# Modulation work taken off GpSimd, and PSUM tiles of two banks, in a two-layer hybrid decoder trunk

## Chip, cores, metric

The kernel runs on one core of a Trainium2 chip. The metric is the device time in microseconds (us) of one execution, from inputs in device memory to the output written there. Lower is better. TensorE, VectorE, ScalarE, GpSimd and SyncE are the engines; in rows they are PE (PEld for its weight loads), DVE, ACT, POOL and SP.

## What is computed

Two layers over one sequence of 256 tokens with 1024 channels, in float32. Each layer has six modulation vectors of 1024 numbers, made from the condition vector `c`; then a mixer (a state space model, differential attention and block attention side by side), and an MLP with a hidden width of 4096:

```python
mod = silu_c @ w_ada[l] + b_ada[l]
sh1, sc1, g1, sh2, sc2, g2 = jnp.split(mod[:, None, :], 6, axis=-1)
h = rmsnorm(x, norm1_g[l]) * (1.0 + sc1) + sh1
proj = h @ w_in[l]
u, dq, dk, dv, mq, mk, mv = jnp.split(proj, splits, axis=-1)
...                                     # y_ssm, y_diff, y_moba
x = x + g1 * (jnp.concatenate([y_ssm, y_diff, y_moba], axis=-1) @ w_out[l])
h = rmsnorm(x, norm2_g[l]) * (1.0 + sc2) + sh2
x = x + g2 * (jnp.square(jax.nn.relu(h @ mlp_w1[l])) @ mlp_w2[l])
```

After the two layers `x` is normalized once more and multiplied by `final_g`.

## The kernel before

**Layout.** `x` stands transposed in SBUF as eight tiles `xT[k]` of 128 channels by 256 tokens. All large weights, 184 units of 128x1024 numbers (512 KB), are read once each, in the order of their use, on SyncE's DMA queue. `unit` (L112) brings one into the ring `raw` (three buffers), ScalarE copies its high part, rounded to the matmul's input format, into `whl` (L118; four buffers), and VectorE writes the rest, raw minus high, beside it (L119). `mm3` (L124, its matmul is L127) multiplies in three terms: high x high, high x low, low x high. So each unit costs a DMA, a ScalarE pass, a VectorE pass and TensorE's work.

**Modulation.** A vector is a sum over eight 128x1024 tiles of `w_ada`, each weighted by eight columns of `cs` (silu of `c`). The tiles come through the ring `ada` (four buffers), also on SyncE's queue (L255), between the raw units. The first two vectors of layer 0 are made at the start; ten come later, each by one of three ways. On TensorE, `ada_two` multiplies two tiles in a step (L250); `ada_finish` transposes the row into a column (L229). On VectorE, `ada_one` does one `scalar_tensor_tensor` per tile (L281; `adaacc` is the accumulator). With `gp`, ScalarE scales the tile (L275) and GpSimd adds it (L277). In the last two ways eight small matmuls sum the accumulator over the partitions (L286). Two vectors go over TensorE, five over VectorE (four from `ada_todo_dve`, one from `ada_todo_last`) and three over GpSimd.

**PSUM.** It has eight banks of 128x512 numbers: four tiles `acc` and four tiles `wk`, one bank each. Projections and the mixer's output accumulate in `acc`; transpositions, sums and other short things use `wk`.

**MLP.** It runs in two halves of 2048 hidden channels. In a half, eight calls of `mlp1_mm` produce a pair of hidden tiles each (two units, 48 matmuls, two `wk` tiles). `p_norm` multiplies each of the two by the row of token norms `rb` on VectorE (L465, 128x258: the last two columns carry the shift); `mlp1_act` does relu, square, the high copies (ScalarE) and the low subtractions (VectorE, L1018) into tiles of other names that are free then (`HID`: `mx`, `at_e`, `uT`, `g2`, `at_on`, `vv`). Then eight calls of `mlp2` each use two units and all 16 hidden tiles (L1035, L1041), in one `acc` tile, and add into `xT[f]` (L1044). In the second half `square_in` sums squares for the next norm on GpSimd (L1058, L1060), and in layer 0 `p_tile` (L450) prepares the next mixer's input; its two 128x2 columns are GpSimd's (L454, L455), its low part is VectorE's (L458).

**Order.** The program is written in the order of two strings `MIXER`, one for each layer's mixer: each word is a piece (P a modulation step on TensorE, D two on VectorE, G on GpSimd, S, Y, O the state space model, C, R, E, V, W, F the attentions, K the output projection). A scheduler then places instructions on their engines by priority; `:n` and `LATE` shift the priority of a piece or of modulation steps. Each engine, and SyncE's queue, runs its instructions in that order.

Of the kernel before, what the change touches and what calls it, by code (L numbers as in the profile page):

```python
# [56 lines left out]
def hybrid_trunk(ctx, tc, xT_d, pos_d, par_d, sb_d, sbt_d, scw_d, glu_d, wm_d, wa_d, out_d):  # L57
# [267 lines left out]

    ada_todo = [(l, i, k) for l, i in ADA_PE for k in range(0, 8, 2)]
    ada_todo_dve = [(l, i, k, 0) for l, i in ((0, 2), (1, 0), (1, 1), (1, 2)) for k in range(8)]
    ada_todo_gp = [(l, i, k, 1) for l, i in ((0, 5), (1, 3), (1, 4)) for k in range(8)]
    ada_todo_last = [(1, 5, k, 0) for k in range(8)]
# [53 lines left out]
    def x_ssq():  # L383

        qs = []
        for i in range(0, KT, 4):
# [996 lines left out]
```

## Time and profile before

| | |
|---|---|
| median of three runs | 711.23 us (710.13 to 718.77) |
| the profiled execution | 710.69 us, of which the span of the trace is 709.0 |
| TensorE busy | 668.0 us, 94% |
| VectorE busy | 565.3 us, 80% |
| ScalarE busy | 423.5 us, 60% |
| GpSimd busy | 96.4 us, 14% |

The span falls into five stages: the start (0 to 56 us: first modulation and first projections), the mixer of layer 0 (56 to 173), its MLP (173 to 393), the mixer of layer 1 (393 to 516) and its MLP (516 to 709). Times in the rows further down count from the start of the span. An engine's busy share is an average over stages with different limits, so rows by stage and the waits of the engine that is busiest are read beside it. "A <- B: total, times, longest" is the time in which A stood idle until B's instruction ended.

### The profile page before, as it was taken

What the parts mean: (1) busy time and instruction counts of PE and PEld (TensorE: products, weight loads), DVE (VectorE), ACT (ScalarE), POOL (GpSimd) and SP (SyncE); (2) the same over time, 40 slices, a digit from 0 to 9 for tenths busy, and PEclk for the clock granted to TensorE, in tenths of its full rate; (3) what the DMA queues carried; (4) which work ended last, traced back from release to release, by engine and by line L of the source; (5) the groups of instructions that cost most, each with busy time, mean ns of one, the idle gap of its engine ahead of it and who ended that gap; (6) DMA issues with size and microseconds to landing.
All of it is one profiled execution on the core that took longest, in us unless ns stands there. A gap on an engine that the chain in (4) does not pass through costs nothing.

```text
span 709.0 us, 13373 instructions
## 1 busy us (share of the span) xinstructions
PE 668.0 (94%) x5046; PEld 593.2 (84%) x5046; DVE 565.3 (80%) x1202; ACT 423.5 (60%) x789; POOL 96.4 (14%) x93
## 2 busy tenths in 40 slices
PE   8999999599999899979699999999999999999994
PEld 6686777588999789979599977788999988999884
DVE  6789989979999897889699888897786566666653
ACT  4568465556777853778544546556577733577540
POOL 0000000911132130134511000001000000000221
PEclk9899999989999999999899999999999999999998
DMA  9986867667787588877686352323455555555531
GB/s 327 395 293 239 307 226 282 242 198 255 241 298 242 184 297 284 315 258 260 252 277 218 122 179 91 124 91 114 149 167 188 178 176 184 183 183 190 188 119 61
DMA packets 42977, 151.98 MB, mean 214 GB/s; under 512 B 4896, under 2 KB 5024, under 8 KB 42912
## 3 DMA queue, kind: packets, MB, share of 16 engines
q1 hardware_dynamic: 42480, 150.60, 61.9%
q8 instruction: 40, 0.66, 0.4%
q10 hardware_dynamic: 432, 0.53, 0.2%
q14 instruction: 25, 0.20, 0.1%
HBM read 150.06 MB, written 1.05 MB: 213 GB/s over the span
## 4 chain that ended last, share of the span: by engine, by line
PE 53%; DVE 21%; DMA 12%; ACT 7%; issue 6%; POOL 1%; SPq 0%; DVEq 0%; ACTq 0%; POOLq 0%
PE wk L127 13%; PE acc L1041 12%; PE acc L127 8%; PE acc L1035 7%; DMA ada<-in_wa_dram 6%; DVE whl L119 6%; DMA raw<-in_wm_dram 4%; DVE adaacc L281 2%; ACT whl L118 2%; PE wk L886 1%; PE wk L286 1%; PE acc L1038 1%; DMA xall<-in_xT_dram 1%; PE acc L812 1%; PE acc L813 1%
## 5 line engine op out<-in xcount | busy, mean ns | idle before, releaser
L118 ACT ACTIVATE whl<-raw 128x1024 fp32r<-128x1024 f32 x184 | 193.8, 1056 | 161.3 <-PE acc L1035 62.9
L119 DVE TENSOR_TENSOR whl<-raw,whl 128x1024 fp32r<-128x1024 f32 x184 | 233.9, 1277 | 64.3 <-ACT whl L118 62.3
L127 PE MATMUL wk<-hx,whl 128*128 128x258 f32 x1536 | 189.9, 285 | 4.9 <-DVE whl L119 4.9
L127 PEld LDWEIGHTS wk<-hx,whl 128*128 128x128 f32 x1536 | 187.4, 191 | 7.2 <-DVE whl L119 5.3
L277 POOL TENSOR_TENSOR qT<-qT,ada 128x1024 f32<-128x1024 f32 x21 | 59.4, 2831 | 150.8 <-ACT ada L275 136.7
L1041 PE MATMUL acc<-mx,whl 128*128 128x512 f32 x240 | 63.6, 409 | 0.0
L281 DVE SCALAR_TENSOR_TENSOR adaacc<-ada,cs,adaacc 128x1024 f32<-128x1024 f32 x35 | 55.1, 1575 | 5.1 <-DMA ada<-in_wa_dram 5.1
L1041 PEld LDWEIGHTS acc<-mx,whl 128*128 128x128 f32 x240 | 45.0, 197 | 8.5
L127 PE MATMUL acc<-mx,whl 128*128 128x256 f32 x384 | 50.5, 289 | 0.0
L127 PEld LDWEIGHTS acc<-mx,whl 128*128 128x128 f32 x384 | 47.8, 194 | 1.6 <-issue 1.4
L1044 DVE SCALAR_TENSOR_TENSOR xall<-acc,mod,xall 128x256 f32<-128x256 f32 x62 | 29.8, 481 | 19.0 <-PE acc L1035 18.2
L127 PE MATMUL acc<-whl,hx 128*128 128x256 f32 x288 | 39.9, 286 | 0.0
L1011 ACT ACTIVATE sp_pa<-sp_pa 128x256 f32<-128x256 f32 x64 | 31.4, 498 | 14.0 <-DVE sp_pa L465 13.8
L812 PE MATMUL acc<-whl,hx 128*128 128x512 f32 x96 | 39.1, 407 | 0.3 <-DVE whl L119 0.3
L127 PEld LDWEIGHTS acc<-whl,hx 128*128 128x128 f32 x288 | 36.4, 189 | 2.8 <-issue 1.6
L813 PE MATMUL acc<-whl,hx 128*128 128x512 f32 x96 | 38.6, 402 | 0.0
L454 POOL CAST hx<-mod 128x2 fp32r<-128x2 f32 x24 | 10.3, 427 | 208.1 <-DVE at_ra L907 120.7
L811 PE MATMUL acc<-whl,hx 128*128 128x512 f32 x96 | 38.5, 406 | 0.0
L1035 PEld LDWEIGHTS acc<-mx,whl 128*128 128x128 f32 x256 | 34.8, 189 | 2.6
L1035 PE MATMUL acc<-mx,whl 128*128 128x256 f32 x256 | 35.6, 281 | 0.0
L465 DVE TENSOR_TENSOR sp_pa<-wk,rb 128x258 f32<-128x258 f32 x64 | 26.5, 419 | 9.2 <-PE wk L127 9.2
L1041 PE MATMUL acc<-at_e,whl 128*128 128x512 f32 x120 | 32.6, 393 | 0.0
(378 smaller groups left out, 1100.3 us busy)
## 6 DMA issues: line engine op xcount, KB each, us to landing
raw<-in_wm_dram SPq DMA_DIRECT2D x184, 512.0 KB, 4.1
ada<-in_wa_dram SPq DMA_DIRECT2D x90, 512.0 KB, 5.9
qT<-in_wa_dram SPq DMA_DIRECT2D x4, 512.0 KB, 8.2
xall<-in_xT_dram SPq DMA_DIRECT2D x4, 256.0 KB, 6.5
adaacc<-in_wa_dram SPq DMA_DIRECT2D x2, 512.0 KB, 9.3
sp_gc<-in_sbt_dram SPq DMA_DIRECT2D x2, 256.0 KB, 4.8
sp_gc<-in_scw_dram SPq DMA_DIRECT2D x2, 256.0 KB, 5.7
sb<-in_sb_dram SPq DMA_DIRECT2D x2, 256.0 KB, 5.1
```

Source lines behind the costliest of these rows:

```text
L118: A.activation(hi, w, AF.Copy)
L119: (eng or V).tensor_tensor(lo, w, hi.bitcast(F32), op=OP.subtract)
L127: last_mm[0] = T.matmul(out, a[:, p, :], b[:, q, :], start=start and i == 0, stop=stop and i == 2, skip_group_check=True)
L277: GP.tensor_tensor(acc, acc, w, op=OP.add)
L281: V.scalar_tensor_tensor(acc, w, c, acc, op0=OP.mult, op1=OP.add)
L811: T.matmul(o, h[:, 0, sl], w[:, 0, :], start=(k == 0), stop=False, skip_group_check=True)
L812: T.matmul(o, h[:, 0, sl], w[:, 1, :], start=False, stop=False, skip_group_check=True)
L813: last_mm[0] = T.matmul(o, h[:, 1, sl], w[:, 0, :], start=False, stop=last, skip_group_check=True)
L1011: A.activation(r[:, i, :S], r[:, i, :S], AF.Relu, bias=r[:, i, S:S + 1])
L1035: last_mm[0] = T.matmul(acc[:, :S], w[:, 1, sl], a[:, 0, :], start=False, stop=last, skip_group_check=True)
L1041: T.matmul(acc, w[:, 0, sl], a.rearrange("p c t -> p (c t)"), start=first, stop=False, skip_group_check=True)
L1044: V.scalar_tensor_tensor(xT[f], acc[:, c * S:(c + 1) * S], mvec(l, 5, f), xT[f], op0=OP.mult, op1=OP.add)
```

## The change

1. `ada_one` has no GpSimd way any more. Vectors (0,3), (0,4) and (1,4) go over TensorE, by steps of four tiles (`ada_four`); (0,2), (0,5), (1,0), (1,1), (1,2), (1,3) and (1,5) over VectorE. VectorE does 8 of its 56 steps in the first mixer, 32 in the MLP of layer 0 (24 before), 8 in the second mixer (none before) and 8 in the MLP of layer 1 (as before). Vector (1,4) on TensorE falls into the second mixer. `LATE` is 60 instead of 100.
2. `p_tile`'s two columns and `square_in`'s sums are VectorE's.
3. `acc` is two tiles of two banks. `mlp1_mm` accumulates a pair in one such tile, `mlp2` in a `wk` tile. `p_norm` is one instruction of 128x516 for a pair, and for 14 of 16 hidden tiles of a half the high copy and the low subtraction are one instruction for a pair, into tiles of double size.
4. The squares for the MLP's norm come first, their sums after the first row of `mlp1_mm`'s matmuls, the norm after the third.
5. The two `MIXER` strings are written in another order, with priorities.

```diff
     def acc_tile():
-        return psum.tile([128, 512], F32, name="acc")
+        return psum.tile([128, 2, 512], F32, name="acc", bufs=2)
...
-    ADA_PE = ((0, 3), (0, 4))
+    ADA_PE = ((0, 3), (0, 4), (1, 4))
...
-    def ada_two(l, i, k):
+    def ada_four(l, i, k):
...
         row = ada_st[l, i]
-        for j in range(2):
-            ada_mm(row, k + j, [ada_tile(l, i, k + j)])
-        if k == 6:
+        ws = [ada_tile(l, i, k + j) for j in range(4)]
+        for j in range(4):
+            ada_mm(row, k + j, ws[j:j + 1])
+        if k == 4:
             ada_fin.append(lambda: ada_finish(l, i, row))
...
-        if gp:
-            A.activation(w if k else acc, w, AF.Copy, scale=c)
-            if k:
-                GP.tensor_tensor(acc, acc, w, op=OP.add)
-        elif k == 0:
+        if k == 0:
             V.tensor_scalar(acc, w, c, None, op0=OP.mult)
         else:
             V.scalar_tensor_tensor(acc, w, c, acc, op0=OP.mult, op1=OP.add)
...
-        GP.tensor_copy(h[:, 0, S:], sh)
-        GP.tensor_tensor(h[:, 1, S:], sh, h[:, 0, S:].bitcast(F32), op=OP.subtract)
+        V.tensor_copy(h[:, 0, S:], sh)
+        V.tensor_tensor(h[:, 1, S:], sh, h[:, 0, S:].bitcast(F32), op=OP.subtract)
...
         t = work.tile([128, 2, SX], F32, name="sp_pa", bufs=2)
-        for i in range(2):
-            V.tensor_tensor(t[:, i], ps[i][:, :SX], rb, op=OP.mult)
+        V.tensor_tensor(t, ps[:, :, :SX], rb[:, None, :].to_broadcast([128, 2, SX]), op=OP.mult)
...
     def mlp1_mm(h, then=None):
-        ps = [wk_tile(), wk_tile()]
+        ps = acc_tile()
...
-            if then and (m, k) == (1, 2):
+            if then and m and k in then:
                 with tc.issue_after(last_mm[0].ins):
-                    then()
+                    then[k]()
...
+        if m < 14:
+            pool, n, bufs = HID[m // 2]
+            a = pool.tile([128, 2, 2, S], F32R, name=n, bufs=bufs)
+            last_act[0] = A.activation(a[:, :, 0, :], r, AF.Copy)
+            last_dve[0] = V.tensor_tensor(a[:, :, 1, :], r, a[:, :, 0, :].bitcast(F32), op=OP.subtract)
+            return [a[:, 0], a[:, 1]]
...
-        acc = acc_tile()
+        acc = wk_tile()
...
-            GP.tensor_scalar(sqsum[0], q, EPS * D / 128, None, op0=OP.add)
+            V.tensor_scalar(sqsum[0], q, EPS * D / 128, None, op0=OP.add)
         else:
-            GP.tensor_tensor(sqsum[0], sqsum[0], q, op=OP.add)
+            V.tensor_tensor(sqsum[0], sqsum[0], q, op=OP.add)
...
-    LATE = 100
+    LATE = 60
...
-    GP_STEPS = (1, 1, 1, 1, 2, 2, 2, 2, 1, 1, 1, 1, 2, 2, 0, 0)
-    V_STEPS = (1, 2, 2, 2, 2, 2, 2, 2, 2, 2, 2, 2, 1, 0, 0, 0)
+    V_STEPS = ((2, 2, 2, 2, 3, 3, 3, 3, 1, 1, 1, 1, 3, 3, 2, 0), (2, 2, 2, 2) + (0,) * 12)
```

The second word string begins, before and now, with "Rm S0 S1 C0 Y0 R0 E01" and "Rm:80 S0:-50 S1:10 C0 P1 Y0 R0 D1 Em0".

What moves on the engines is seen at two places. First, VectorE at the first pairs of the MLP of layer 0. Its rows before, from the end of the norm (L405 to L407 write `rb`) to the first hidden tiles (`mx`):

```order
L281 SCALAR_TENSOR_TENSOR adaacc<-ada,cs,adaacc 128x1024
L406 TENSOR_TENSOR so_y<-so_y,sq 128x256
L119 TENSOR_TENSOR whl<-raw,whl 128x1024
L407 SCALAR_TENSOR_TENSOR rb<-so_y,sq 128x256
L119 TENSOR_TENSOR whl<-raw,whl 128x1024
L465 TENSOR_TENSOR sp_pa<-wk,rb 128x258 x3
L119 TENSOR_TENSOR whl<-raw,whl 128x1024
L281 SCALAR_TENSOR_TENSOR adaacc<-ada,cs,adaacc 128x1024
L465 TENSOR_TENSOR sp_pa<-wk,rb 128x258
L1018 TENSOR_TENSOR mx_2333<-sp_pa,mx_2333 128x256
L1018 TENSOR_TENSOR mx_2336<-sp_pa,mx_2336 128x256
L281 SCALAR_TENSOR_TENSOR adaacc<-ada,cs,adaacc 128x1024
L465 TENSOR_TENSOR sp_pa<-wk,rb 128x258
```


and now (L278 is the modulation step, L409 to L411 the end of the norm, L468 `p_norm`, L1017 the subtraction):

```order
L409 SCALAR_TENSOR_TENSOR so_y<-wk,sq 128x256
L278 SCALAR_TENSOR_TENSOR adaacc<-ada,cs,adaacc 128x1024
L410 TENSOR_TENSOR so_y<-so_y,sq 128x256
L278 SCALAR_TENSOR_TENSOR adaacc<-ada,cs,adaacc 128x1024
L411 SCALAR_TENSOR_TENSOR rb<-so_y,sq 128x256
L119 TENSOR_TENSOR whl<-raw,whl 128x1024
L468 TENSOR_TENSOR sp_pa<-acc,rb 128x516
L119 TENSOR_TENSOR whl<-raw,whl 128x1024 x2
L1017 TENSOR_TENSOR mx_2305<-sp_pa,mx_2305 128x2x256
L468 TENSOR_TENSOR sp_pa<-acc,rb 128x516
L278 SCALAR_TENSOR_TENSOR adaacc<-ada,cs,adaacc 128x1024
L119 TENSOR_TENSOR whl<-raw,whl 128x1024
```


The pair's four VectorE instructions (two L465, two L1018) have become two of double size, in `acc` instead of `wk`, and between two norms there stand two steps and two weight subtractions.

Second, SyncE's queue from the end of the MLP of layer 0 into the second mixer. Its rows before, where L255 brings a modulation tile and L110 a unit of the large weights:

```order
L255 DMA ada<-in_wa_dram 128x1024 x2
L110 DMA raw<-in_wm_dram 128x1024
L255 DMA ada<-in_wa_dram 128x1024 x2
L110 DMA raw<-in_wm_dram 128x1024 x3
L255 DMA ada<-in_wa_dram 128x1024
L110 DMA raw<-in_wm_dram 128x1024 x93
```


and now, where the row of 18 units runs from the last three of the MLP of layer 0 to the fifteenth of the second mixer's 28:

```order
L255 DMA ada<-in_wa_dram 128x1024
L110 DMA raw<-in_wm_dram 128x1024 x18
L255 DMA ada<-in_wa_dram 128x1024 x6
L110 DMA raw<-in_wm_dram 128x1024 x3
L255 DMA ada<-in_wa_dram 128x1024 x4
L110 DMA raw<-in_wm_dram 128x1024
L255 DMA ada<-in_wa_dram 128x1024 x2
L110 DMA raw<-in_wm_dram 128x1024
L255 DMA ada<-in_wa_dram 128x1024
```


Before, the last 93 units, the second mixer's among them, follow one another with no modulation tile between; now batches of six and four tiles and smaller ones stand between the units of the second mixer.

## Rows read from the trace of the kernel before

**Rows 1.** The page: busy time of each engine, share of the span, instructions.

```profile
PE 668.0 (94%) x5046; PEld 593.2 (84%) x5046; DVE 565.3 (80%) x1202; ACT 423.5 (60%) x789; POOL 96.4 (14%) x93
```

**Rows 2.** Windows: length, busy us of PE, PEld, DVE, ACT, POOL; clock, DMA share, GB/s.

```profile
56.00:173.00 117.00, 107.53 (x899) 87.41 (x892) 105.21 (x268) 68.65 (x162) 23.99 (x22) 0.97 0.72 252
173.00:393.00 220.00, 206.26 (x1477) 190.75 (x1476) 194.38 (x256) 144.38 (x226) 56.45 (x38) 0.97 0.75 261
393.00:516.00 123.00, 118.45 (x948) 102.20 (x946) 101.76 (x291) 74.36 (x177) 4.06 (x16) 1.00 0.38 121
412.00:495.00 83.00, 78.45 (x666) 65.55 (x665) 70.75 (x233) 49.49 (x134) 4.06 (x16) 1.00 0.36 115
```

**Rows 3.** TensorE's waits from 56 to 186 us: total, times, longest.

```profile
PE wk L958 <- DVE at_on L953: 8.4, 2, 8.1
```

**Rows 4.** TensorE's waits from 186 to 395 us, same columns.

```profile
PE acc L1041 <- DVE at_on L1018: 7.9, 2, 5.9
PE wk L127 <- DVE whl L119: 4.9, 2, 2.7
PE acc L1041 <- DVE uT L1018: 0.5, 1, 0.5
```

**Rows 5.** Windows behind the waits, columns as in rows 2; PEclk is the granted clock.

```profile
142.70:148.00 5.30, 5.30 (x34) 5.30 (x35) 3.80 (x8) 2.49 (x5) 0.00 (x0) 0.71 0.50 157
...
344.40:350.50 6.10, 6.10 (x19) 5.19 (x20) 3.37 (x5) 3.16 (x5) 1.45 (x2) 0.50 0.17 67
```

**Rows 6.** Timeline of VectorE, mixer 0: start, duration, instruction.

```profile
130.88 1.87 DVE L946 TENSOR_TENSOR at_ms<-at_q,at_r 128x4 f32<-128x4 f32 x1
...
134.20 2.19 DVE L140 TENSOR_TENSOR rs_t<-rs_i 128x4 f32<-128x4 f32 x1
...
136.82 0.16 DVE L140 TENSOR_TENSOR rs_t<-rs_i 128x4 f32<-128x4 f32 x1
...
137.42 2.23 DVE L140 TENSOR_TENSOR rs_t<-rs_i 128x4 f32<-128x4 f32 x1
...
139.88 2.19 DVE L142 SCALAR_TENSOR_TENSOR at_rq<-rs_t,rs_i 128x4 f32<-128x4 f32 x1
```

**Rows 7.** Timeline of GpSimd and VectorE, MLP 0.

```profile
308.56 5.92 POOL L277 TENSOR_TENSOR qT<-qT,ada 128x1024 f32<-128x1024 f32 x2 [16.63 <-ACT ada L275]
...
309.14 3.09 DVE L119 TENSOR_TENSOR whl<-raw,whl 128x1024 fp32r<-128x1024 f32 x1
...
312.16 3.41 DVE L281 SCALAR_TENSOR_TENSOR adaacc<-ada,cs,adaacc 128x1024 f32<-128x1024 f32 x1
...
315.83 1.27 DVE L281 SCALAR_TENSOR_TENSOR adaacc<-ada,cs,adaacc 128x1024 f32<-128x1024 f32 x1
```

**Rows 8.** Lines by form: count, then busy us, mean ns, idle time before.

```profile
L119 DVE TENSOR_TENSOR whl<-raw,whl 128x1024 fp32r<-128x1024 f32 x184 | 233.9, 1277 | 64.3 <-ACT whl L118 62.3
L281 DVE SCALAR_TENSOR_TENSOR adaacc<-ada,cs,adaacc 128x1024 f32<-128x1024 f32 x35 | 55.1, 1575 | 5.1 <-DMA ada<-in_wa_dram 5.1
L465 DVE TENSOR_TENSOR sp_pa<-wk,rb 128x258 f32<-128x258 f32 x64 | 26.5, 419 | 9.2 <-PE wk L127 9.2
L719 DVE TENSOR_TENSOR sp_gc<-sp_s,tb_c 128x512 f32<-128x512 f32 x8 | 5.5, 684 | 0.0
L277 POOL TENSOR_TENSOR qT<-qT,ada 128x1024 f32<-128x1024 f32 x21 | 59.4, 2831 | 150.8 <-ACT ada L275 136.7 <-PE wk L423 13.9
```

**Rows 9.** Window in MLP 1, VectorE's L119 alone: busy us (count).

```profile
516.00:608.00 92.00, 40.07 (x33) 1.00 0.57 184
```

**Rows 10.** The chain that ended last: start, duration, instructions.

```profile
84.45 1.00 PE wk L250 x16
...
114.01 0.54 PE wk L229 x4
...
518.34 43.19 PE wk L127 x359
...
561.53 1.68 PE wk L286 x16
```

More of the change, by code (lines that the diff above doesn't have):

```diff
@@ L324, in ada_first @@
         return sums
[L326 to L329, printed above, removed]
+    ada_todo = [(l, i, k) for l, i in ADA_PE for k in range(0, 8, 4)]
+    ada_todo_dve = [(l, i, k) for l, i in ((0, 2), (0, 5), (1, 0), (1, 1), (1, 2), (1, 3), (1, 5)) for k in range(8)]
     def ada_step(n):
@@ L388, in x_ssq, with x_ssq_sum @@
             qs += [q[:, j, :] for j in range(4)]
+        for k in range(6):
+            A.activation(qs[k], xT[k], AF.Square)
+        return qs
+    def x_ssq_sum(qs):
         ps = ssq_begin()
         for k in range(6):
-            ssq_add(ps, xT[k], k, 6, qs[k])
+            g = k % 4
+            last_mm[0] = T.matmul(ps[32 * g:32 * g + 32, :], ones, qs[k], start=(k < 4), stop=(k >= 2),
+                                  tile_position=(0, 32 * g), skip_group_check=True)
         p6 = work.tile([128, S], F32, name="sq", bufs=3)
@@ L803, in add @@
                 if self.kind == "p":
-                    mm3(self.ps[i][:, :SX], w[:, :, sl], h, k == 0, last)
+                    mm3(self.ps[:, i, :SX], w[:, :, sl], h, k == 0, last)
                 elif self.kind == "u":
@@ L996, in mlp1_mm @@
         for m, k in order:
-            mm3(ps[m][:, :SX], us[m][:, :, k * 128:k * 128 + 128], h[k], k == 0, k == KT - 1)
-            if then and (m, k) == (1, 2):
+            mm3(ps[:, m, :SX], us[m][:, :, k * 128:k * 128 + 128], h[k], k == 0, k == KT - 1)
+            if then and m and k in then:
                 with tc.issue_after(last_mm[0].ins):
-                    then()
+                    then[k]()
         return ps
-    HID = [(big, f"mx{i}", 1) for i in range(8)] + [(work, "at_e", 4)] * 4 + \
-        [(big, "uT", 1), (work, "g2", 1), (work, "at_on", 1), (work, "vv", 2)]
+    HID = [(big, f"mx{i}", 1) for i in range(4)] + [(work, "qT", 3)] * 3
     def mlp1_act(ps, m):
@@ L1155, in hybrid_trunk @@
     for l in range(L):
-        mixed = [big.tile([128, 2, S], F32R, name=f"mx{k}") for k in range(KT)]
+        mixed = [big.tile([128, 2, 2, S], F32R, name=f"mx{k}") for k in range(KT // 2)]
+        mixed = [m[:, i] for m in mixed for i in range(2)]
         if l == 0:
@@ L1205, in hybrid_trunk @@
                 if not accs:
-                    accs = [acc_tile() for _ in range(4)]
+                    accs = [acc_tile() for _ in range(2)]
                 back_unit(accs, mixed[mix[a]], a == "m", False)
@@ L1217, in hybrid_trunk @@
             pts.append(p_tile(l, f, ag[:, f:f + 1], 3))
-        sq = x_ssq()
+        qs, sq = x_ssq(), []
         slot = 0
@@ L1224, in hybrid_trunk @@
                 if i < 8:
-                    acts += mlp1_act(mlp1_mm(pts, None if half or i else lambda: x_norm(*sq)), 2 * i)
+                    acts += mlp1_act(mlp1_mm(pts, None if half or i else {0: lambda: sq.append(x_ssq_sum(qs)), 2: lambda: x_norm(*sq.pop())}), 2 * i)
                 else:
@@ L1248, in hybrid_trunk @@
                         with tc.issue_after(last_dve[0].ins), tc.issue_after(last_act[0].ins):
-                            todo.pop(0)()
+                            for f in todo[:1]:
+                                f()
+                        todo = todo[1:]
                     elif j == 12:
```

61 lines of the change are left out of this document (27 added, 34 removed).

## The prediction

> **What bounds the kernel now.** I read the page's first part, then the windows by stage, then TensorE's waits in them, then the timelines around the waits. TensorE is busy for 668.0 of 709.0 us [rows 1], and its matmuls follow each other with few gaps, so time can come only from its few long waits, from stretches at a lower clock, and from matmuls added or removed. VectorE is the next one: 105.2 of 117 us in the first mixer, 194.4 of 220 in the MLP of layer 0, but 70.8 of 83 in the middle of the second mixer (the four rows are the first mixer, the MLP of layer 0, the second mixer, and its middle; [rows 2]). GpSimd works almost only in the first two of these (24.0 and 56.5 us).
>
> The long waits stand there too. In the first mixer TensorE waits 8.4 us for VectorE's `at_on` [rows 3]; in the MLP of layer 0 it waits 7.9 us for `at_on` (a half of the middle layer's last pair, L1018), 4.9 us for the low parts of weights (`whl`) and 0.5 us for `uT` [rows 4]. Just behind the waits the granted clock falls: means of 0.71 over 5.3 us in the mixer, and in the MLP, over three stretches, 0.63 over 4.6, 0.66 over 5.0 and 0.50 over 6.1 (the first and the last of the four are in [rows 5]). A stretch of length t at mean clock c costs t(1-c): 1.5 us in the mixer, and 1.7+1.7+3.1 = 6.5 us in the MLP.
>
> Why is VectorE late? In the chain before the first `at_on`, instructions of 128x4 take 2.19 us where the same line and form takes 0.16 [rows 6]. In the MLP, while two GpSimd additions (L277) run from 308.56 to 314.5, a weight subtraction (L119) takes 3.09 us and a modulation step (L281) 3.41; the next L281, behind them, takes 1.27 [rows 7]. In a stretch of the MLP of layer 1 that has no L277, L119 takes 40.07/33 = 1.214 us [rows 9]. Against these clean prices the L281 lose 55.1-35x1.27 = 10.7 us and the L119 lose 233.9-184x1.214 = 10.5 us over the run [rows 8]. The normalization L465, which has one input in PSUM, has a mean of 419 ns in the same stages [rows 8]. So I read the long ones as VectorE held up while GpSimd reads SBUF beside it, for as long as one L277 lasts (2.83 us, [rows 8]).
>
> **The change, part by part.** The sum goes against the profiled execution's 710.69 us, 0.5 under the median of 711.23.
>
> *GpSimd's 24 additions go.* First mixer: the chain of the 8.4 us wait holds four long ones of 1.87 to 2.23 us [rows 6]; each comes down to 0.16, which is 7.8 us of the wait. With the lower clock behind it: -9.3. Bounds: -4 (the reordered mixer string makes a smaller wait there) and -10. MLP of layer 0: the waits are 7.9+4.9+0.5 = 13.3, the clock behind them 6.5, so -19.8. Two sums over partitions leave this stage (six vectors end in it before, four after), each 16 records of small matmuls, 1.68 us [rows 10]: -3.4.
>
> *What VectorE gets for it in that MLP.* Eight more steps (32 for 24) at 1.27 us are 10.2; 16 pairs of 128x2 operations that were GpSimd's, at 0.16 (the nearest form, 128x4, [rows 6]), are 5.1; seven sums of squares of 128x256 at about the 0.42 of L465 are 2.9. Taken off: the merged normalization is one 128x516 instruction for two of 128x258. No row shows it; 128x512 on SBUF takes 0.684 (L719), two L465 take 0.838 [rows 8], so it lies between these; I take 0.69, since what is saved is one fixed cost, and 16 pairs give 2.4. Merged subtractions give about as much, 28 x 0.15 = 4.2 over the two layers, 2.1 here. So VectorE's load is 194.4 - 21 (the two groups above, nearly all of it here) + 10.2 + 5.1 + 2.9 - 4.5 = 187, and less by what other lines lose beside L277. TensorE's stream is 206.3 - 6.5 - 3.4 = 196.4 [rows 2]. VectorE fits, but at 95%, so some waits for `whl` should stay: I take +3, with bounds of 0 and 12 (nearly all of the 13.3 comes back). The MLP of layer 0: -19.8-3.4+3 = -20.2.
>
> ScalarE's 24 scalings go as well, and four merged instructions a pair; TensorE waits for ScalarE nowhere long in these stages, so both count nothing. The MLP of layer 1 has eight steps before and after: nothing.
>
> *Second mixer.* It has no modulation work before; now it has one vector on TensorE and eight steps on VectorE. TensorE: the 16 records of one step of two tiles (a matmul of f32 leaves two records) take 1.00 us, so eight tiles 4.0; the transposition behind them 0.54; the sum of the vector that VectorE ends here 1.68 [rows 10]: +6.2, with nothing beside it since TensorE is the stream. VectorE: 10.2 for the steps and 16 operations of 128x2, 2.6, together 12.8; idle there are 12.2 of the 83 us in the middle and 21.2 of all 123 [rows 2]. The attention chains of this stage go through VectorE, so steps that get in front of them show. Bounds: 6.2 (all hidden) to 19.0 (all in line). I take about a third of VectorE's part as shown: +10. The loads come in batches on SP's queue, six `ada` tiles for four buffers, so raw weights stand behind a wait for VectorE; 28 units in 123 us are 4.4 us each, and seven buffers (three `raw`, four `whl`) cover 30 us: nothing. The DMA share of 0.36 leaves room [rows 2].
>
> *Two PSUM tiles of two banks.* Sixteen pairs in each layer. A pair's 48 matmuls take 5.77 us (359 in 43.19, so 0.1203 each, [rows 10]). There are two pairs of buffers before and after; but before, the first bank of a pair is free after its own 0.42 us, and its normalization may start 8.2 us after that bank's last matmul. Now the norm must start within 5.77-0.69 = 5.1 us of the pair's end. VectorE's own work for a pair is two L119, one step, norm and subtraction: 2.43+1.27+0.69+0.68 = 5.07 us, under 5.77. Nothing, as long as this holds. Order of squares and sums at the start of the MLP: about 1 us either way, taken as nothing.
>
> **Sum:** 710.7 - 9.3 - 20.2 + 10 = **691.2 us**.
>
> **The rivals.**
>
> *The second mixer takes all added work in line*: 19.0 for 10, 700. For it: the chains through VectorE. Against it: 21 us of idle VectorE.
>
> *It hides the steps and no wait stays in the MLP*: 710.7-9.3-23.2+6.2 = 684. For it: the steps have lower priority than the chain. Against it: 95% load.
>
> *The pairs become the bound* (this ends on the other side). If VectorE comes to a norm later than 5.1 us after its pair, the next-but-one pair of matmuls waits, in PSUM's place rather than the weights'. Three L119 and three steps ahead of a norm are 7.4 us, so 2.3 us a pair; over layer 0's 16 pairs that is 37 us, 728. It decides from 1.2 us a pair (19.5/16). For it: the order shows up to two L119, two steps and a subtraction between two norms (5.6 us). Against it: that many only now and then, since the steps are about one a pair. The Trainium skill has a rule on this side (Perfetto Trace Analysis, Optimizing Scalar/DVE Operations): where Vector isn't saturated but makes other engines idle, breaking instructions up may let work end sooner; the merge does the reverse, and by the rule two norms of half the size would be better here. No run yet shows which.
>
> *The long instructions aren't GpSimd's doing* (the change doesn't do what it says). Then mixer and MLP keep their waits, VectorE gets 13.7 us more (10.2+5.1+2.9-4.5) in a stage where it is already late, and the second mixer adds 10: 710.7-3.4+10 = 717 if the new work still finds gaps, to 731. For it: other causes of a 3 us subtraction can't be seen. Against it: [rows 6, 7], and that L465 is never long.
>
> **How the numbers follow.** The main course 0.60, with a range of its own of 685 to 699; all in line in the second mixer 0.16; all hidden 0.12; the pairs 0.09; not GpSimd 0.03. 80% lie between 681 and 705: what is left out is most of the last two and the ends of the second. A change of 2% (about what can be told from no change) is at 697.0 and 725.5. Faster: nine tenths of the main course, the hidden case, a fifth of the second: 0.69. Slower: half of the last two and some worse mixtures: 0.08. The rest, 0.23, lies within.
>
> **What the profile after would show.** Right: no L119 or L278 (the step's new line) over 1.5 us; the wait for `at_on` in the first mixer under 1 us; waits in the MLP of layer 0 under 4 us in all, and no granted clock under 0.9 there; the MLP of layer 0 near 200 us for 220; the second mixer near 133 for 123. Wrong: TensorE waiting at the first matmuls of a pair for VectorE's norm; the second mixer longer by 15 us or more; long VectorE instructions with GpSimd silent; or the new first mixer, whose pieces stand in another order, waiting somewhere else for as long as before.

## The result, and the profile after

The changed kernel takes **683.62 us** (median of four runs, 682.83 to 686.71) for 711.62 of the kernel before; the ratio is 0.959, with a 95% interval of 0.953 to 0.965. 691.2 was predicted, with a range of 681 to 705, so the direction and the range held, and the gain of 28 us was 8 us larger than the 20 forecast. Some terms of the sum were further off than the total, as the stages show.

The profile is that of the slowest of the four runs (686.71; its span is 684.8). First the page: the busy time of each engine, then the granted clock of TensorE in 40 slices.

```profile
PE 666.2 (97%) x5098; PEld 591.1 (86%) x5098; DVE 543.4 (79%) x1219; ACT 394.5 (58%) x738; POOL 3.1 (0%) x10
...
PEclk9998599999999999999999999999999999999998
```

Against [rows 1], TensorE does about the same work in 24 us less, GpSimd does almost nothing, and VectorE's busy time has fallen by 22 us though it has taken over work. One slice, the fifth, stands at half clock.

To compare stages I cut both spans where the first matmul of the MLP of layer 0, of the second mixer, and of the MLP of layer 1 starts:

| us | before | changed | difference | predicted |
|---|---|---|---|---|
| start and first mixer | 175.7 | 171.3 | -4.4 | -9.3 |
| MLP of layer 0 | 217.3 | 193.7 | -23.6 | -20.2 |
| second mixer | 120.0 | 122.8 | +2.8 | +10 |
| MLP of layer 1 and end | 196.0 | 197.0 | +1.0 | 0 |
| span | 709.0 | 684.8 | -24.2 | -19.5 |

The windows of the two middle stages before (length, busy us of PE, PEld, DVE, ACT and POOL with counts, clock, DMA share, GB/s):

```profile
175.70:393.00 217.30, 203.91 (x1467) 190.08 (x1467) 191.71 (x250) 141.68 (x220) 56.45 (x38) 0.97 0.75 260
393.00:513.00 120.00, 115.45 (x924) 99.59 (x922) 98.76 (x283) 71.36 (x169) 4.06 (x16) 1.00 0.39 124
```

and the same two of the changed kernel:

```profile
171.30:365.00 193.70, 193.70 (x1444) 181.87 (x1443) 166.77 (x244) 123.34 (x192) 0.00 (x0) 1.00 0.76 259
365.00:487.80 122.80, 121.65 (x1000) 104.39 (x999) 106.25 (x307) 70.46 (x167) 0.00 (x0) 1.00 0.58 193
```

In the MLP of layer 0 TensorE is now busy for all of 193.7 us, at full clock throughout: the waits of [rows 4] and the low-clock stretches of [rows 5] are gone. In the second mixer it has 6.2 us more work, the figure of the sum, and the stage is only 2.8 us longer. What is left of its waits of 0.5 us and more, from 45 to 172 us and from 365 to 490 (total, times, longest):

```profile
PE wk L250 <- DMA ada<-in_wa_dram: 3.0, 4, 1.3
```

```profile
PE wk L858 <- DVE qk L854: 0.7, 2, 0.5
```

The wait of 8.4 us for `at_on` [rows 3] is gone too, but a wait of 3.0 us for modulation tiles has come in its place. The lines of VectorE that answer to [rows 8] (L278 is the modulation step, L468 the norm of a pair):

```profile
L119 DVE TENSOR_TENSOR whl<-raw,whl 128x1024 fp32r<-128x1024 f32 x184 | 224.2, 1222 | 54.8 <-ACT whl L118 53.0
L278 DVE SCALAR_TENSOR_TENSOR adaacc<-ada,cs,adaacc 128x1024 f32<-128x1024 f32 x49 | 62.7, 1279 | 0.9 <-DMA ada<-in_wa_dram 0.7
L468 DVE TENSOR_TENSOR sp_pa<-acc,rb 128x516 f32<-128x516 f32 x33 | 22.8, 692 | 6.0 <-PE acc L127 6.0
```

L119 has a mean of 1.22 us and the step one of 1.28 (priced at 1.214 and 1.27), and the norm that no row showed takes 0.692 us, for the 0.69 taken.

### The profile page after: what moved, and what is told of

It reads as the page before. It is cut to its first block, busy times and chain, and to the rows that moved or that the text cites. A ratio compares the mean times of both kernels' runs of the same rounds, so it can differ in the third digit from the quotient of the medians.

```text
span 684.8 us, 13240 instructions
## 1 busy us (share of the span) xinstructions
PE 666.2 (97%) x5098; PEld 591.1 (86%) x5098; DVE 543.4 (79%) x1219; ACT 394.5 (58%) x738; POOL 3.1 (0%) x10
## 3 DMA queue, kind: packets, MB, share of 16 engines
HBM read 150.06 MB, written 1.05 MB: 221 GB/s over the span
## 4 chain that ended last, share of the span: by engine, by line
PE 82%; DVE 10%; DMA 5%; ACT 2%; issue 1%; DVEq 0%; SPq 0%; ACTq 0%
PE acc L127 37%; PE wk L1046 16%; PE wk L1040 9%; DMA ada<-in_wa_dram 3%; DVE whl L119 3%; PE acc L813 2%; PE acc L811 2%; PE wk L886 2%; PE acc L812 2%; PE wk L283 2%; PE wk L705 1%; PE wk L250 1%; PE wk L1043 1%; ACT whl L118 1%; PE wk L925 1%
## 5 line engine op out<-in xcount | busy, mean ns | idle before, releaser
L119 DVE TENSOR_TENSOR whl<-raw,whl 128x1024 fp32r<-128x1024 f32 x184 | 224.2, 1222 | 54.8 <-ACT whl L118 53.0
L127 PE MATMUL acc<-hx,whl 128*128 128x258 f32 (+1 forms) x1632 | 202.4, 284 | 0.0
L127 PEld LDWEIGHTS acc<-hx,whl 128*128 128x128 f32 x1632 | 198.6, 190 | 4.1 <-issue 3.8
L278 DVE SCALAR_TENSOR_TENSOR adaacc<-ada,cs,adaacc 128x1024 f32<-128x1024 f32 x49 | 62.7, 1279 | 0.9 <-DMA ada<-in_wa_dram 0.7
L1046 PE MATMUL wk<-mx,whl 128*128 128x512 f32 x240 | 61.1, 394 | 0.0
L127 PE MATMUL acc<-mx,whl 128*128 128x256 f32 x384 | 51.4, 288 | 0.0
L1046 PEld LDWEIGHTS wk<-mx,whl 128*128 128x128 f32 x240 | 42.9, 188 | 7.8
L127 PEld LDWEIGHTS acc<-mx,whl 128*128 128x128 f32 x384 | 47.5, 191 | 2.1 <-issue 1.8
L1046 PE MATMUL wk<-qT,whl 128*128 128x512 f32 x180 | 47.0, 398 | 0.0
L1049 DVE SCALAR_TENSOR_TENSOR xall<-wk,mod,xall 128x256 f32<-128x256 f32 x62 | 29.9, 482 | 15.6 <-PE wk L1040 14.7
L1040 PEld LDWEIGHTS wk<-mx,whl 128*128 128x128 f32 x256 | 34.8, 190 | 2.4
L1046 PEld LDWEIGHTS wk<-qT,whl 128*128 128x128 f32 x180 | 32.0, 190 | 5.3
L1040 PE MATMUL wk<-mx,whl 128*128 128x256 f32 x256 | 35.7, 282 | 0.0
L1040 PEld LDWEIGHTS wk<-qT,whl 128*128 128x128 f32 x192 | 27.0, 188 | 2.6
```

The lines of the kernel that those rows point to most:

```text
L119: (eng or V).tensor_tensor(lo, w, hi.bitcast(F32), op=OP.subtract)
L127: last_mm[0] = T.matmul(out, a[:, p, :], b[:, q, :], start=start and i == 0, stop=stop and i == 2, skip_group_check=True)
L278: V.scalar_tensor_tensor(acc, w, c, acc, op0=OP.mult, op1=OP.add)
L1040: last_mm[0] = T.matmul(acc[:, :S], w[:, 1, sl], a[:, 0, :], start=False, stop=last, skip_group_check=True)
L1046: T.matmul(acc, w[:, 0, sl], a.rearrange("p c t -> p (c t)"), start=first, stop=False, skip_group_check=True)
L1049: V.scalar_tensor_tensor(xT[f], acc[:, c * S:(c + 1) * S], mvec(l, 5, f), xT[f], op0=OP.mult, op1=OP.add)
```

## The experiments

The theory: GpSimd's additions hold VectorE up, the hold-ups make TensorE's waits, and these bring the low clock behind them. The rivals: the gain comes from the new order and the merged instructions; or VectorE's long instructions have another cause. Times are medians of at least four runs; ratios are to the kernel before on the same chip. A table of the stages of all runs stands at the end of this section.

### GpSimd's additions left out of the kernel before (`b_nogp`)

```diff
             A.activation(w if k else acc, w, AF.Copy, scale=c)
             if k:
-                GP.tensor_tensor(acc, acc, w, op=OP.add)
+                pass
```

> The kernel before, with GpSimd's 21 modulation additions (L277) left out; ScalarE still scales their tiles, so three modulation vectors hold one tile in place of eight. Nothing else moves. Theory (GpSimd's reads of SBUF hold VectorE up, and these hold-ups make the waits): the waits for at_on in the first mixer and in the MLP of layer 0 and most of the wait for whl go, no L119 or L281 over 1.5 us stays; 682 to 692 us. Rival (the change's gain comes from its new order and its merged instructions): within 4 us of the kernel before, long VectorE instructions stay.

Measured: **681.76 us** (680.51 to 684.11; ratio 0.957, 0.953 to 0.961). With no other edit this is the time of the changed kernel. L119 in the kernel before and here (the three numbers are the shortest, median and longest, in ns):

```profile
L119 DVE TENSOR_TENSOR whl<-raw,whl x184: 1196/1224/3159, 17.9 to 688.8; 128x1024 fp32r<-128x1024 f32 x184
```

```profile
L119 DVE TENSOR_TENSOR whl<-raw,whl x184: 1199/1225/1229, 17.6 to 658.7; 128x1024 fp32r<-128x1024 f32 x184
```

and the window of the MLP of layer 0 here:

```profile
164.70:363.10 198.40, 196.77 (x1468) 185.01 (x1468) 166.88 (x250) 140.62 (x220) 16.13 (x23) 1.00 0.82 285
```

The same 250 VectorE instructions take 166.9 us for 191.7: 24.8 us were lost in this stage alone, and the stage is 18.9 us shorter (19.8 were worked out from the waits and the clock). The first mixer is 11.0 us shorter, for 9.3; TensorE waits 0.6 us for `at_on` there, for 8.4, and the chain in front of it has lost its long instructions of 128x4 (L140 before, then here):

```profile
L140 DVE TENSOR_TENSOR rs_t<-rs_i x18: 151/161/2231, 98.2 to 490.4; 128x4 f32<-128x4 f32 x12, 128x8 f32<-128x8 f32 x6
```

```profile
L140 DVE TENSOR_TENSOR rs_t<-rs_i x18: 153/162/169, 97.8 to 460.2; 128x4 f32<-128x4 f32 x12, 128x8 f32<-128x8 f32 x6
```

The first rival falls as the main cause. One step over the 1.5 us of the expectation is left; GpSimd's sums of squares, which stay in this run, have to do with it (last section).

### The additions moved to VectorE, in the order of before (`b_dve`)

```diff
-        if gp:
-            A.activation(w if k else acc, w, AF.Copy, scale=c)
-            if k:
-                GP.tensor_tensor(acc, acc, w, op=OP.add)
-        elif k == 0:
+        if k == 0:
             V.tensor_scalar(acc, w, c, None, op0=OP.mult)
```

> The kernel before, with the 24 GpSimd steps done as VectorE steps at the same places of the program, and without ScalarE's scalings; order and PSUM as before. Theory: VectorE gains the hold-ups back (at least 21 us) and pays 24 steps of 1.27 us (30 us); in the MLP of layer 0 it then carries about 190 of some 205 us, so part of the waits stays, for whl and hidden tiles: 690 to 702 us. Rival (hold-ups not GpSimd's doing): 711 plus the added load, 720 to 740. Rival (moving the additions is the whole gain, order and PSUM tiles give nothing): 681 to 686, as the changed kernel.

Measured: **696.49 us** (693.94 to 697.89; ratio 0.976, 0.972 to 0.981). The window of the MLP of layer 0, and TensorE's first wait from 50 to 182 us:

```profile
182.20:380.30 198.10, 196.71 (x1471) 184.99 (x1468) 182.61 (x265) 125.18 (x203) 17.61 (x23) 1.00 0.80 279
```

```profile
PE wk L954 <- DVE at_on L949: 6.6, 2, 6.3
```

The MLP is as long as with the additions left out (198.1 for 198.4), although VectorE does 182.6 us of work there: at 92% it still hides under TensorE. In the first mixer steps stand between the links of the attention's chain (four of 1.28 us in the 12 us ahead of `at_on`), the wait for `at_on` is back with 6.6 us, and the granted clock is 0.80 on the mean from 125 to 175 us. So the moving alone gives 16 us of the 31 that leaving out gives on this chip; the rest depends on where the steps are put. The time fell in the range expected, but for another reason: the waits stayed in the mixer, not in the MLP.

### GpSimd set to work again beside the changed kernel (`a_gpnoise`)

The lines stand at the end of `ada_one`; `noise[0]` is 24 at the start of the MLP of layer 0:

```diff
+        if noise[0] > 0:
+            noise[0] -= 1
+            GP.tensor_tensor(w, w, w, op=OP.add)
```

> The changed kernel, with a GpSimd addition of 128x1024 (a modulation tile doubled in place after VectorE has used it, which changes no result) behind each of the first 24 VectorE steps of the MLP of layer 0. Theory: VectorE instructions with two SBUF inputs that fall beside one of these 24 take up to 3.4 us again, VectorE's busy time in this MLP grows by 20 to 35 us, and the waits come back: 692 to 710 us. Rival (VectorE's long instructions had another cause): 682 to 687 us.

Measured: **720.30 us** (715.39 to 724.95; ratio 1.011, 1.005 to 1.017), more than expected. The timeline of GpSimd, then of VectorE, in the MLP of layer 0:

```profile
175.46 2.01 POOL L290 TENSOR_TENSOR ada<-ada 128x1024 f32<-128x1024 f32 x1 [10.27 <-DVE adaacc L280]
178.63 2.01 POOL L290 TENSOR_TENSOR ada<-ada 128x1024 f32<-128x1024 f32 x1 [1.16 <-DVE adaacc L280]
```

```profile
174.10 1.28 DVE L280 SCALAR_TENSOR_TENSOR adaacc<-ada,cs,adaacc 128x1024 f32<-128x1024 f32 x1
...
175.63 2.92 DVE L280 SCALAR_TENSOR_TENSOR adaacc<-ada,cs,adaacc 128x1024 f32<-128x1024 f32 x1
...
178.80 2.91 DVE L119 TENSOR_TENSOR whl<-raw,whl 128x1024 fp32r<-128x1024 f32 x1
```

A VectorE instruction that starts 0.17 us behind a GpSimd one takes 2.9 us instead of 1.2 or 1.3. Both end 1.08 us after the GpSimd instruction does (175.63+2.92 against 175.46+2.01, and the same below). So do all 17 L119 and L280 of this trace that start while an addition runs, though they have between 1.2 and 1.8 us of it ahead of them: VectorE waits for the end of it, and only then does its own work. This is the cause put back, and the last rival falls for the long instructions. VectorE is busy 31.6 us longer in this MLP (198.4 for 166.8), and the stage takes 227.6 us for 193.7. How much of these 33.9 us is VectorE's hold-up is not shown: the additions also keep modulation tiles from being freed, and SyncE's queue waits for that (166 to 393.6 us), which no run here separates:

```profile
SPq L255 <- POOL ada L290: 39.5, 13, 5.3
```

What instruction is held up shows in the line of the norm, which has one input in PSUM and one in SBUF:

```profile
L473 DVE TENSOR_TENSOR sp_pa<-acc,rb 128x516 f32<-128x516 f32 x33 | 22.8, 690 | 3.2 <-PE acc L127 3.2
```

Its mean is 690 ns, as without GpSimd, and the longest takes 697; two of the 33 run beside an addition. In the kernel before, six L465 run beside an L277, and none of all 64 takes over 428 ns. The Trainium skill says the same (SBUF — State Buffer, Who interferes with whom): VectorE with two inputs in SBUF contends with a GpSimd instruction that reads SBUF, and with at most one, outside its 2-port modes, it doesn't. The traces agree. TensorE's waits, 160 to 394 us:

```profile
PE acc L127 <- DVE sp_pa L473: 7.4, 5, 3.8
PE wk L285 <- DVE adaacc L280: 5.9, 1, 5.9
PE wk L1051 <- DVE vv L1028: 5.4, 2, 4.2
```

The first is the rival of the pairs: once VectorE is late, TensorE waits for the norm that frees a pair's PSUM tile. It shows only where VectorE is late.

### The norm in two instructions (`a_norm2`)

```diff
-        V.tensor_tensor(t, ps[:, :, :SX], rb[:, None, :].to_broadcast([128, 2, SX]), op=OP.mult)
+        for i in range(2):
+            V.tensor_tensor(t[:, i], ps[:, i, :SX], rb, op=OP.mult)
```

> The changed kernel, with the norm of a pair in two VectorE instructions of 128x258 on the same PSUM tile of two banks. Theory: 33 pairs cost 33 x 0.15 = 5 us more of VectorE, hidden under TensorE, since no norm is waited for: 682 to 686 us. Rival (breaking the instruction up lets work end sooner): 675 to 681. Rival (VectorE so full that its load shows): 686 to 690.

Measured: **684.48 us** (679.69 to 685.39; ratio 0.959, 0.954 to 0.964): no difference. The 66 halves take 421 ns each, and the MLP of layer 0 is 193.7 us long in both. The merge saves VectorE 25.1-22.8 = 2.3 us net, all hidden; breaking the instruction up gains nothing either, since no norm is waited for.

```profile
L469 DVE TENSOR_TENSOR sp_pa<-acc,rb 128x258 f32<-128x258 f32 x66 | 25.1, 421 | 5.6 <-PE acc L127 5.6
```

### The changed kernel again (`a_again`)

> The changed kernel itself once more, for a second profile and as the base for the runs of this group. 682 to 686 us. In the first profile the granted clock was 0.50 from 65 to 80 us; if that belongs to the order of the first mixer it is there again, if it was this one execution it is not.

Measured: **681.77 us** (679.70 to 683.93; ratio 0.957, 0.954 to 0.960). The first mixer ends at 167.3 us in this profile, for 171.3 in the other, and all later stages agree within 0.2 us. The clock falls again, but to 0.50 from 60 to 70 us only (65 to 80 in the other profile).

### Two other starts of the first mixer (`a_late`, `a_two`)

The first words of the first string, in the changed kernel, in `a_late`, and in `a_two` (where a P is a step of two tiles, as before, and later P are doubled):

```diff
-D2:-10 P1 P1 Rm S0:10 Em1 Em0 S1 C0 Y0 R0
+P1 Rm S0:10 Em1 Em0 S1 C0 D2:-10 P1 Y0 R0
+D2:-10 P2 Rm S0:10 Em1 Em0 P1 S1 C0 Y0 P1 R0
```

> The changed kernel, with the start of the first mixer's string as 'P1 Rm S0 Em1 Em0 S1 C0 D2 P1 Y0 R0' in place of 'D2 P1 P1 Rm S0 Em1 Em0 S1 C0 Y0 R0': the first two VectorE steps and the second step on TensorE come behind three raw units on SyncE's queue. Theory (TensorE's waits for modulation tiles between 54 and 69 us, where six tiles come in a row, bring the lower clock behind them): the 3 us of waits shrink to under 1.5 and the clock stays above 0.9 from 60 to 85 us; 673 to 679 us. Rival (the clock falls there for another reason, or the tiles are waited for later in the same way): 682 to 686.

Measured: **689.12 us** (685.64 to 690.52; ratio 0.967, 0.965 to 0.970): worse than either case. The waits for modulation tiles are down to 0.2 us, but TensorE waits 4.2 us for `qk` (L854), and the clock is again 0.50 from 60 to 65 us. From 53.7 to 56.8 us, just ahead of the attention's rotation (L851 to L854), VectorE works on the tables of the state space model (L607 to L609); no weight subtraction stands there. The loss moved.

> The changed kernel, with steps of two tiles on TensorE as before, the first four tiles at the start of the first mixer's string and the next four in two single steps after Em0 and Y0; the second mixer's as pairs of steps where the single ones stood. Theory (as for the late one): smaller batches are waited for less, 675 to 681. Rival (batches don't matter): 682 to 686.

Measured: **678.37 us** (678.29 to 680.59; ratio 0.953, 0.950 to 0.956), 3.4 us under `a_again` on the same chip. The intervals overlap by 0.002, so that it is faster is likely, not shown. Two windows of the changed kernel (first profile), then of `a_two`:

```profile
55.00:60.00 5.00, 2.47 (x28) 0.89 (x28) 4.94 (x17) 5.00 (x12) 0.00 (x0) 1.00 0.89 304
65.00:70.00 5.00, 5.00 (x27) 2.46 (x21) 2.56 (x8) 3.26 (x4) 0.00 (x0) 0.50 1.02 413
```

```profile
55.00:60.00 5.00, 2.52 (x31) 0.89 (x28) 4.97 (x17) 5.00 (x11) 0.00 (x0) 1.00 0.96 337
65.00:70.00 5.00, 4.91 (x31) 3.49 (x30) 5.00 (x23) 4.35 (x8) 0.00 (x0) 1.00 1.00 395
```

TensorE is idle for half of 55 to 60 us in both; the waits for tiles are 2.5 us for 3.0. What differs is the clock behind it: 0.50, the lower of the two levels (1.2 GHz), in the one, 1.00 in the other. So the smaller batches did not do what the theory said of them, and why the clock held is open. It held in the profile of `a_best` too, which has this start, and also in that of `a_gpnoise`, which has the changed kernel's.

### The start in the order of before (`a_start`)

The first words of the first string, in `a_two` and here:

```diff
-D2:-10 P2 Rm S0:10 Em1 Em0 P1 S1 C0 Y0 P1 R0
+P2 S0 Rm P1 D2 Em1 S1 C0 Em0 P1 Y0 R0
```

> The kernel with steps of two tiles (a_two), and the start of the first mixer's string in the order of before: 'P2 S0 Rm P1 D2 Em1 S1 C0 Em0 P1 Y0 R0' in place of 'D2 P2 Rm S0 Em1 Em0 P1 S1 C0 Y0 P1 R0'. Two raw units instead of one then stand ahead of the modulation tiles on SyncE's queue. Theory (TensorE stood idle for half of 55 to 60 us because its modulation tiles and the next raw unit came late, and this is the only part of the first mixer that is worse than before): it is busy for over 4 us in that window, no clock below 0.9, the first mixer ends 1 to 3 us earlier; 675 to 678 us. Rival (the loss there is shifted to the next wait for tiles or weights): 678 to 683.

Measured: **684.86 us** (681.96 to 688.08; ratio 0.960, 0.956 to 0.965): the rival's mechanism, and slower than either case. TensorE is busy for 3.28 us from 55 to 60 (2.52 in `a_two`), but for 1.72 only in the next five; there are waits of 1.3 us for modulation tiles (at 57), 1.3 for `whl` (at 61) and 2.4 for `qk` (at 64).

### The second mixer without modulation work (`a_nomod1`), and without VectorE's part of it (`a_novec`)

In `a_nomod1` all P and D are taken out of the second string, which begins:

```diff
-Rm:80 S0:-50 S1:10 C0 P1 Y0 R0 D1 Em0
+Rm:80 S0:-50 S1:10 C0 Y0 R0 Em0
```

In `a_novec` the string stays, and `ada_one` leaves seven steps out:

```diff
-        if k == 0:
+        if (l, i) == (1, 3) and k:
+            pass
+        elif k == 0:
             V.tensor_scalar(acc, w, c, None, op0=OP.mult)
```

> The changed kernel, with the second mixer's modulation work left out: vectors (1,3) and (1,4) are set to zero, so eight VectorE steps, eight tiles on TensorE and one sum over partitions are missing. Theory (VectorE's steps are hidden, TensorE's part is not): 6 to 7 us less, 676 to 678. The prediction's own +10 would give 673 to 675; all in line, 663 to 667.

Measured: **686.94 us** (684.58 to 690.81), slower with less work. The edit moved other instructions as well: TensorE waits for a tile of the second mixer's input that it did not wait for before, and a lower clock follows (0.66 on the mean from 370 to 380 us).

```profile
PE acc L811 <- ACT hx L443: 4.3, 1, 4.3
```

So this run prices nothing. The next one keeps every place:

> The changed kernel, with seven of the second mixer's eight VectorE steps left out (vector (1,3) holds one tile only); their tiles are still loaded, TensorE's part, the sum over partitions and all places in the program stay. This prices VectorE's share of the second mixer, which the prediction put at +4. Theory (hidden): the stage stays within 1 us of 123. Prediction: 4 us shorter. All in line: 9 us shorter.

Measured: **686.99 us** (680.43 to 693.30; ratio 0.958, 0.952 to 0.965); with runs 13 us apart the total settles nothing. The stage of the second mixer with the steps (`a_again`) and without seven of them:

```profile
361.00:484.00 123.00, 121.72 (x1001) 104.47 (x1000) 106.31 (x307) 70.55 (x167) 0.00 (x0) 1.00 0.57 193
```

```profile
363.80:487.80 124.00, 121.50 (x1000) 104.25 (x999) 101.05 (x300) 70.21 (x167) 0.00 (x0) 1.00 0.56 191
```

VectorE does 5.3 us less and the stage is no shorter (124.0 us for 123.0). The seven steps cost nothing there.

### The second mixer in the order of before (`a_oldmix1`)

The second string's first half:

```diff
-Rm:80 S0:-50 S1:10 C0 P1 Y0 R0 D1 Em0 Vm E01:30 D1:60 Em1 E00:10 S2 P1 D1 Wm0:-30 Wm1 C1 D1:30
+Rm S0 S1 C0 P1 Y0 R0 D1 E01 D1 E00 Em0 Vm Em1 S2 P1 D1 Wm0 Wm1 C1 D1
```

> The changed kernel, with the second mixer's pieces in the order of before and without priorities; the two TensorE pieces and eight VectorE pieces stand between them about where they stood. Theory (the new order of the second mixer took away the waits of 4 us that the stage had, which is why the stage grew by 3 us only for 6.8 us more of TensorE's work): the stage takes 126 to 129 us for 123. Rival (the order does nothing, the prediction's price was just too high): 122 to 124.

Measured: **694.22 us** (691.41 to 698.10; ratio 0.973, 0.969 to 0.977). Some of this is a first mixer of 174.5 us with a long half-clock stretch. The second mixer takes 125.9 us (126 to 129 expected) for 122.9, with waits that the new order mostly doesn't have:

```profile
PE wk L858 <- DVE qk L854: 1.4, 3, 0.8
PE wk L930 <- DVE at_eT L927: 1.0, 2, 0.7
PE wk L886 <- DVE at_m L891: 1.0, 1, 1.0
PE acc L127 <- DVE mx L962: 0.7, 1, 0.7
```

So the new order of this stage is worth 3 us. It isn't what hides the steps: in the old order without modulation work (the kernel before) the stage took 120.0 us, and with all of it it takes 125.9, which is no more than TensorE's added 6.2. The new order takes away waits that the stage had before the change, 4.3 us in all from 393 to 513.

### Vector (1,4) on VectorE (`a_best`, on the base of `a_two`)

```diff
-    ADA_PE = ((0, 3), (0, 4), (1, 4))
+    ADA_PE = ((0, 3), (0, 4))
...
-    V_STEPS = ((2, 2, 2, 2, 3, 3, 3, 3, 1, 1, 1, 1, 3, 3, 2, 0), (2, 2, 2, 2) + (0,) * 12)
+    V_STEPS = ((2, 2, 2, 2, 4, 4, 4, 4, 2, 2, 2, 2, 3, 3, 2, 0), (2, 2, 2, 2) + (0,) * 12)
```

> The kernel with steps of two tiles (a_two), and vector (1,4) on VectorE instead of TensorE: 40 steps in the MLP of layer 0, eight in the second mixer. TensorE loses eight tiles and a transposition (4.5 us) and gets a sum (1.7), VectorE gets 10 us more in the MLP of layer 0, where it is busy for 167 of 194 us. If VectorE still fits there: 675 to 676. If the pairs begin to wait for VectorE's norms: 678 to 690.

Measured: **697.11 us** (695.50 to 699.74; ratio 0.977, 0.974 to 0.980). Neither case: the sum of a vector over the partitions stands at a fixed place in TensorE's order, and the last step now comes 5.8 us behind it.

```profile
PE wk L283 <- DVE adaacc L278: 5.8, 1, 5.8
```

The MLP of layer 0 takes 206.2 us for 195.1, and the second mixer, 126.3 us long, has the wait of `a_nomod1` as well. The removal of an estimated 2.8 us (4.5 less 1.7) from TensorE cost 19.

### All runs by stage

| us | time | first mixer ends | MLP 0 | mixer 1 |
|---|---|---|---|---|
| before | 711.6 | 175.7 | 217.3 | 120.0 |
| changed | 683.6 | 171.3 | 193.7 | 122.8 |
| `a_again` | 681.8 | 167.3 | 193.7 | 122.9 |
| `b_nogp` | 681.8 | 164.7 | 198.4 | 119.8 |
| `b_dve` | 696.5 | 182.2 | 198.1 | 120.0 |
| `a_gpnoise` | 720.3 | 166.0 | 227.6 | 122.9 |
| `a_norm2` | 684.5 | 169.8 | 193.7 | 123.0 |
| `a_two` | 678.4 | 164.0 | 195.1 | 122.8 |
| `a_late` | 689.1 | 169.5 | 194.0 | 123.2 |
| `a_start` | 684.9 | 165.6 | 194.8 | 123.1 |
| `a_nomod1` | 686.9 | 166.6 | 193.7 | 125.6 |
| `a_novec` | 687.0 | 170.1 | 193.7 | 124.0 |
| `a_oldmix1` | 694.2 | 174.5 | 195.1 | 125.9 |
| `a_best` | 697.1 | 163.9 | 206.2 | 126.3 |

The stages are those of the one profiled execution, the time is the median of all. Six rows with the same first mixer as the changed kernel (`a_again`, `a_gpnoise`, `a_norm2`, `a_nomod1`, `a_novec`, `a_oldmix1`) end it between 166.0 and 174.5 us.

## Why the prediction was right, and where it was not

**GpSimd holds VectorE up, and that makes the waits: right.** `b_nogp` takes it away and `a_gpnoise` puts it back; each moves the time as the reading of [rows 6, 7] says. The price from the waits and the clock behind them (9.3 and 19.8 us) was close: 11.0 and 18.9 without the additions. The signs of this part came: no L119 or L278 over 1.3 us, no wait for `at_on` in the first mixer, and in the MLP of layer 0 no wait and a granted clock of 1.00.

**Which course came.** The main course was 685 to 699 us, and 683.62 lies outside it. What came in the MLP of layer 0 and in the second mixer is the rival that hides the steps and leaves no wait in the MLP, which had a chance of 0.12 and gave 684. That its number was met so closely is luck: the second mixer came out 3.4 us better than in that rival, and the first mixer 1 to 5 us worse.

**The MLP of layer 0: -20.2 forecast, -23.6 measured.** The term that failed is the +3 for waits that stay at a load of 95%. None stays, and the load is 166.8 of 193.7 us, 86%. The parts are 18.9 for GpSimd (`b_nogp`), 3.1 of TensorE's work (196.77 to 193.70 us, with 3.4 forecast for two sums), and the 1.6 us of waiting that `b_nogp` still had. Four figures of the load of 187 us were too high or too low. Its start of 194.4 is that of a window from 173 us; the stage itself had 191.7. The loss through GpSimd was 24.8 us there, not 21: I had counted two groups of lines only, which lost 16.7 in this stage, and other lines lost the rest. Of the 16 pairs of 128x2 operations eight run there (2.6 us for 5.1). And, the largest, the eight more steps are one. The prediction took the places of the steps from the program's lists, but the queues decide when they run. The steps (L281) of the kernel before in its MLP of layer 0 and in the rest of its span behind the second mixer:

```profile
175.70:393.00 217.30, 41.48 (x26) 0.97 0.75 260
...
513.00:709.00 196.00, 0.00 (x0) 0.98 0.51 164
```

and of the changed kernel (L278):

```profile
171.30:365.00 193.70, 34.50 (x27) 1.00 0.76 259
...
487.80:684.80 197.00, 8.96 (x7) 0.99 0.52 172
```

The vector written for the MLP of layer 1 ran in the MLP of layer 0 before, as SyncE's queue ahead of the prediction shows (no modulation tile among the last 93 units). So "the MLP of layer 1 has eight steps before and after" was wrong for the kernel before: it went from none to seven there. These are not what makes the stage 1 us longer. The whole lines of its windows, before and changed, have the work of TensorE:

```profile
513.00:709.00 196.00, 187.05 (x1327) 175.18 (x1326) 123.77 (x176) 108.60 (x167) 10.51 (x8) 0.98 0.51 164
```

```profile
487.80:684.80 197.00, 188.10 (x1336) 175.66 (x1334) 132.44 (x163) 107.65 (x156) 1.67 (x1) 0.99 0.52 172
```

TensorE has nine records and 1.05 us more, and seven of the nine are sums of squares of the MLP's norm (12 for 5), which the change puts behind the first row of matmuls (its item 4). They crossed the cut between the stages (as in layer 0), so the second mixer is the shorter for them: the 1 us is work moved, not time lost.

**The second mixer: +10 forecast, +2.8 measured.** TensorE's 6.2 us were right (121.65 busy for 115.45; the added lines themselves take 6.9, less what crossed the cut). The step that failed is the third of VectorE's part, +4: `a_novec` prices seven of the eight steps at nothing, and `a_oldmix1` shows no cost in the old order either. And the new order, which the sum had counted nowhere, is worth 3 us (`a_oldmix1`): the waits of the stage fell from 4.3 to 0.7 us.

**The first mixer: -9.3 forecast, -4.4 and -8.4 in two profiles of the changed kernel** (-1.2 to -9.7 in five more with the same first mixer). The wait for `at_on` went as worked out. The bound of -4 named what came: the new string has a wait of its own, of 3.0 us. Six modulation tiles in a row on SyncE's queue and the raw units behind them leave TensorE idle for 2.5 of the five us from 55 on (0.2 before), and in six of the seven profiles a stretch at half clock follows. The prediction's paragraph on SyncE's queue looked at the second mixer only.

**The pairs of PSUM banks: nothing, as taken.** No norm is waited for in the changed kernel, and two norms for one make no difference: 684.5 us for 683.6 and 681.8. The rule of the Trainium skill that the prediction weighed (Perfetto Trace Analysis, Optimizing Scalar/DVE Operations) speaks of instructions that make other engines idle; this one makes none idle here. The rival is real beside a late VectorE (`a_gpnoise`).

**The sum.** +7 too dear for the second mixer, +3.4 for the MLP of layer 0, against 1 to 5 us too much gain in the first mixer and 1 us in the last stage: the errors add to some 5 to 9 us, on the slow side. The mechanism was right; the second mixer's term was 3.6 times what came, the first mixer's up to twice.

## What to carry to other kernels

Look for instructions of one line and one form with two durations, and at what another engine does beside the long ones: leaving GpSimd's additions out gave, in one edit, as much as the whole change. An instruction that ends a fixed time after the other engine's, whenever it began, has waited for it. Work that is moved to a busy engine costs nothing where that engine has slack and no chain, and 15 us where it stands ahead of a chain (`b_dve`); count where the steps run in the trace's queues, not where the program lists them. Both reorderings that took away a wait at the start of the first mixer (`a_late`, `a_start`) brought the next one, so price an order by all engines that it feeds.

## What the runs showed of the hardware that was not expected

An addition that takes GpSimd 2.0 us makes one VectorE instruction 1.6 to 1.7 us longer, more than a VectorE step on a tile of that size takes (1.28 us). VectorE isn't slowed down but kept waiting: the held-up L119 and steps end 1.08 us after GpSimd's instruction, whether 1.2 or 1.8 us of it were left. GpSimd's smaller sums do this too. In `b_nogp` no L119 takes over 1.23 us, but six of the 24 L458 take 0.62 to 0.97 us for 0.48, each beside a sum of 128x256 (L1058, L1060), and one step beside such a sum takes 1.76 us for 1.28; it ends 1.09 us after the sum:

```profile
L458 DVE SCALAR_TENSOR_TENSOR hx<-xall,ag,hx x24: 475/485/967, 161.9 to 484.8; 128x256 fp32r<-128x256 f32 x24
```

```profile
335.69 0.74 POOL L1060 TENSOR_TENSOR sg_t<-sg_t,sq 128x256 f32<-128x256 f32 x1 [6.29 <-ACT sq L1055]
...
335.76 1.76 DVE L281 SCALAR_TENSOR_TENSOR adaacc<-ada,cs,adaacc 128x1024 f32<-128x1024 f32 x1 [0.66 <-DMA ada<-in_wa_dram]
```

So moving `square_in`'s sums to VectorE takes away hold-ups as well; what that is worth in time no run shows.

The same order of the first mixer ran with and without a stretch at half clock behind the same idle time of TensorE. From 55 to 60 us it was busy for 2.38 us in `a_novec` and 2.39 in `a_gpnoise`; from 65 to 70 the clock was 0.50 in the one and 1.00 in the other, and the first mixer ended at 170.1 and 166.0 us. The times of one kernel move with it by about 4 us: `a_again` took 679.70 us at a mean clock of 0.992 and 683.93 at 0.983. `a_two` stayed at 0.990 or above in its four runs. What decides this is open.
